# Two figures of an order model: the issue of wide transfers and matmuls of small tiles, in a two-branch decoder layer

## The chip, the cores and the metric

The kernel runs on one core of a Trainium2 chip. The metric is device time of one execution in microseconds. Three runs of the kernel before gave 1865.16, 1866.49 and 1883.88 us; the median is 1866.49 us.

## The reference

One hybrid decoder layer on 2048 positions of width 1024, batch 1, all in float32. The heart of it, cut:

```python
h = x_ln * (1 + scale(c)) + shift(c)          # layer norm, then modulation by c @ w_ada
proj = h @ w_in                               # 1024 -> 4232 columns
rw = proj[:, :1664]; rw = rw + (shifted(rw) - rw) * mix
# group A, RWKV-7, 8 heads x 64: per position
#   S = S * w_t - (S kk_t)(kk_t * a_t)^T + v_t k_t^T ;  y_t = S r_t
# then a group norm and a bonus term
# group B, forgetting attention, 8 heads x 64, causal, blocks of 128 queries:
#   softmax(q k^T / 8 + cum_t - cum_s) v
y = concat(y_a, y_b) * silu(proj[:, 3208:])
out = layer_norm(2 ** 0.25 * x_ln + (1 + gate(c)) * (y @ w_out)) * ln_g + ln_b
```

## The kernel before, in words

**Tiles.** The positions go in two halves of 1024, each half in two blocks of 512. The projection of a half is 33 weight tiles of 128 columns; each tile and block takes 8 steps over the inner dimension, and each step is three float32r matmuls of 128x128 by 512 columns (high times high, high times low, low times high; `proj_tile`). That makes 3,072 matmuls that read `ht` and `wsp`, besides 96 early ones that read `wx`. The output projection (`final_tile`) is 16 tiles of 128 positions with 48 such matmuls each, 768 in all; they read the same two names. These 3,840 matmuls depend on little: where one of them stands in TensorE's queue, it fills time that a chain would leave.

**Chains.** For each half there is a RWKV stage (`rwkv_stream`: 8 units, each with elementwise work, a triangular solve of small 32x32 matmuls, state steps of 128x64 matmuls, and a post step) and then an attention stage (`fox_stream`). In an attention stage `fox_ops` loads the operands of the heads (`fx_s`) from scratch in DRAM, `fox_guard` computes scores for the row maxima (a matmul into a bank of PSUM, then a reduction on VectorE that frees the bank; at most GI = 3 are in flight), `fox_s` computes the scores again for the exponentials (into `fx_p`), and `fox_pv` multiplies by the values (`fx_v`), two key tiles side by side on the halves of the array. `fox_values` transposes the values out of `arena` tiles that come from `vscr`. The stages are called attention 0 and attention 1 here.

**Ends.** `final_prep` loads `w_ada` and `w_out`, and VectorE and GpSimd scale `w_out` and split it into two parts (it starts when all projections of half 1 have been planned, and the parts take the place of half 1's activations, so when these have been used). Each output tile has an epilogue on VectorE: `final_evac` adds the residual, takes statistics and writes four passes over 128x512 (`SCALAR_TENSOR_TENSOR`), two of which can be read at the end of the program as `end_s<-end_s,small,arena`.

**What sets the order.** All instructions are recorded by generators that a small scheduler, `Driver`, runs in the order of a model's time. Each call of an engine asks `Driver.time`, which takes the cost from `cost` (or, for TensorE, `on_pe`, which keeps a time for each of the 4x4 cells of the array and adds 100 ns where the tile's shape changes) and notes when the result is ready. A generator that yields goes on when the model says that its work is done; free slots and banks are given out by the same clock. So a figure in the model changes no instruction but, by shifting the model's time, which generator goes next, and with it the place of every later instruction in the five in-order queues. The model's figure is never a time on the chip.

Names: `NB` is 512 columns, `pe.free` is when the model's TensorE is free, `LATENCY` is what the model adds behind each engine's end. All recorded instructions carry the line of the recording call (L134), so the profile is read by tile names.

Of the kernel before, what the change touches and what calls it, by code (L numbers as in the profile page):

```python
# [137 lines left out]
class Driver:  # L138
# [31 lines left out]
    def cost(self, e, op, ops, kw):  # L170
        out, ins = ops[0], ops[1:]
        n = max(a.free_size() for a in ops)
        sb = all(a.space != "PSUM" for a in ops)
        if "dma_start" in op:
            return 450.0 if e.name == "sp" else 1000.0
        if e.name == "act":
            return (94 if sb else 51) + 0.834 * n + 93 * sum(isinstance(kw.get(k), bass.AP) for k in ("scale", "bias"))
        if e.name == "dve":
            if op == "reciprocal":
                return 65 + 6.25 * n  # L180
            if op == "tensor_tensor_scan":
                return 69 + 2.15 * n
            if op == "tensor_tensor_reduce":
                return 180 + 1.04 * n
            ptr = 61 * sum(a.free_size() == 1 for a in ins[1:]) if "scalar" in op else 0
            if op in ("tensor_copy", "tensor_scalar", "memset") and sb:
                return 69 + 0.52 * n + ptr
            return 69 + 1.04 * n + ptr
        if op == "affine_select":
            return 137 + 0.834 * n  # L190
        if kw.get("op") == OP.pow:
            return 300 + 165 * n
        return 147 + 2.17 * n if op == "tensor_tensor" else 161 + 0.834 * n if op == "tensor_scalar" else 34 + 0.834 * n
# [17 lines left out]
    def on_pe(self, t, op, ops):  # L211

        m, n, k = ops[1].free_size(), ops[2].free_size(), list(ops[1].ap)[0][1]
        r0, c0 = ops[1].start_partition() // 32, ops[0].start_partition() // 32
        nr, nc = (1 if x <= 32 else 2 if x <= 64 else 4 for x in (k, m))
        one = ops[1].dtype == F32R or op == "transpose"
        stream, load = n * (1 if one else 2) / 2.4, m * 2 / 2.4
        if nr == nc == 4:
            d = max(stream + (14 if n >= 256 else 3), load + 2)
        else:  # L220
            d = max(stream + (load if nc < 4 else 6), 25.0)
        d *= 1 if one else 2
        t = max(t, self.pe.began + 7)
        if (nr, nc) != self.mode:
            t = max(t, max(max(x) for x in self.cells) + (100 if self.mode else 0))
            self.mode = (nr, nc)
        cells = [(i, j) for i in range(r0, min(4, r0 + nr)) for j in range(c0, min(4, c0 + nc))]
        t = max(t, max(self.cells[i][j] for i, j in cells))
        for i, j in cells:
            self.cells[i][j] = t + d  # L230
        self.pe.began = t + (0 if one else 7)
        self.pe.free = max(self.pe.free, t + d)
        return t + d
# [1871 lines left out]
```

## Time and profile before

| What | Value |
|---|---|
| Median of three runs | 1866.49 us |
| The profiled execution's own time | 1866.47 us |
| Its span | 1864.7 us |
| TensorE busy | 1784.5 us, 96% |
| VectorE busy | 1287.4 us, 69% |
| ScalarE busy | 804.4 us, 43% |
| GpSimd busy | 779.3 us, 42% |
| DMA, mean share of 16 engines | 30.6% |
| Granted TensorE clock, mean | 0.98 of 2.4 GHz |

The profiled execution is 0.02 us from the median, and 1.8 us of its time lie outside the span. A busy TensorE is not one at its peak: a matmul counts as busy from its start to its modelled end, and at a granted clock of 0.5 (1.2 GHz) it counts twice as long. A stretch's idle time is its length less TensorE's busy time.

### The profile page before, as it was taken

The numbers are of one execution on the slowest core, as the hardware profiler recorded it, in microseconds if no ns is written. First come the engines' busy times: TensorE is split into PE (matmuls) and PEld (weight loads), VectorE is DVE, ScalarE is ACT, GpSimd is POOL, SyncE is SP. The second block draws the span as 40 slices with busy tenths as digits, with TensorE's granted clock in tenths as the row PEclk, the third lists the DMA queues.
The fourth block names the chain that finished last, engine by engine and source line by source line (L and its number), as shares of the span: only waits on it lengthen the run. The fifth ranks groups of instructions, "written<-read, shape, count | busy, mean of one in ns | idle before, by whom it ended". The sixth has DMA issues, their size and how long they took to land.

```text
span 1864.7 us, 35565 instructions
## 1 busy us (share of the span) xinstructions
PE 1784.5 (96%) x13609; PEld 1288.3 (69%) x13609; DVE 1287.4 (69%) x3049; ACT 804.4 (43%) x1571; POOL 779.3 (42%) x773
## 2 busy tenths in 40 slices
PE   8999999999999899999999999989899899999995
PEld 6777777767777656677777777767555356666884
DVE  4987685665773768667657675762677584876998
ACT  2454555354444245554554554443244344432000
POOL 1333242422423357743143442424256364566652
PEclk8999999998999999999999999999899899999998
DMA  8252020210122755132021120213422732512433
GB/s 263 72 163 81 30 69 23 80 51 26 53 87 86 226 172 178 58 115 84 19 78 36 41 79 30 75 39 114 131 92 84 244 111 77 191 57 90 153 115 122
DMA packets 172129, 181.60 MB, mean 97 GB/s; under 512 B 12180, under 2 KB 116197, under 8 KB 171960
## 3 DMA queue, kind: packets, MB, share of 16 engines
q1 hardware_dynamic: 171960, 179.33, 30.6%
q8 instruction: 108, 1.77, 0.4%
q14 instruction: 61, 0.50, 0.1%
HBM read 132.10 MB, written 47.13 MB: 96 GB/s over the span
## 4 chain that ended last, share of the span: by engine, by line
PE 55%; DVE 5%; ACT 3%; SPq 3%; DMA 2%; issue 2%; POOL 1%; DVEq 0%; ACTq 0%; POOLq 0%
PE ps L134 55%; SPq L134 3%; ACT rw_s L134 2%; DVE rw_s L134 2%; DMA arena<-vscr 1%; DVE end_s L134 1%; DVE small L134 1%; DVE arena L134 1%; POOL rw_s L134 0%; POOL wsp L134 0%; DMA arena<-in_b_ada_dram 0%; ACT arena L134 0%; DMA yscr<-rw_s 0%; DVE fx_p L134 0%; DMA fx_s<-qscr 0%
## 5 line engine op out<-in xcount | busy, mean ns | idle before, releaser
L134 PE MATMUL ps<-ht,wsp 128*128 128x512 f32 x3840 | 976.4, 400 | 3.4 <-POOL wsp L134 1.3
L134 PEld LDWEIGHTS ps<-ht,wsp 128*128 128x128 f32 x3840 | 701.1, 189 | 163.3 <-issue 15.0
L134 POOL TENSOR_TENSOR wsp<-wst,wsp 128x1024 fp32r<-128x1024 f32 x79 | 192.8, 2440 | 320.2 <-ACT wsp L134 256.2
L134 ACT ACTIVATE rw_s<-ps 64x256 f32<-64x256 f32 (+3 forms) x544 | 215.9, 409 | 200.7 <-PE ps L134 101.0
L134 PE MATMUL ps<-fx_s 67*128 67x512 f32 (+6 forms) x960 | 261.1, 390 | 12.3 <-DMA fx_s<-kscr 4.0
L134 ACT ACTIVATE fx_p<-ps 128x512 f32<-128x512 f32 (+3 forms) x336 | 162.8, 521 | 196.2 <-PE ps L134 175.6
L134 PEld LDWEIGHTS ps<-fx_s 67*128 67x128 f32 (+1 forms) x960 | 165.4, 193 | 118.3 <-issue 47.7
L134 POOL TENSOR_TENSOR fx_p<-fx_p 128x512 f32<-128x512 f32 (+2 forms) x160 | 185.7, 1167 | 140.7 <-PE ps L134 138.3
L134 PE MATMUL ps<-rw_s 32*32 32x32 f32 (+4 forms) x5376 | 227.7, 217 | 17.0 <-DVE rw_s L134 8.0
L134 PEld LDWEIGHTS ps<-rw_s 32*32 32x32 f32 (+3 forms) x5376 | 195.7, 130 | 66.1 <-issue 26.6
L134 DVE TENSOR_TENSOR rw_s<-rw_s 128x24 f32<-128x24 f32 (+11 forms) x544 | 179.8, 336 | 26.0 <-ACT rw_s L134 12.6
L134 DVE TENSOR_REDUCE small<-ps 128x1 f32<-128x512 f32 (+1 forms) x208 | 134.5, 683 | 44.4 <-PE ps L134 43.6
L134 ACT ACTIVATE arena<-ps 128x512 f32<-128x512 f32 (+3 forms) x128 | 74.1, 581 | 191.6 <-PE ps L134 161.7
L134 POOL TENSOR_TENSOR small<-small,nhalf 128x8 f32<-128x8 f32 (+1 forms) x48 | 68.3, 1425 | 211.6 <-DVE small L134 211.5
L134 PE MATMUL ps<-fx_p,fx_v 128*64 128x512 f32 (+3 forms) x640 | 155.9, 556 | 0.0
L134 DVE TENSOR_TENSOR fx_p<-fx_p 128x512 f32<-128x512 f32 (+1 forms) x128 | 111.9, 874 | 51.6 <-POOL fx_p L134 48.9
L134 ACT ACTIVATE wsp<-wst 128x1024 fp32r<-128x1024 f32 x80 | 84.3, 1054 | 134.2 <-PE ps L134 110.1
L134 DVE TENSOR_SCALAR state<-ps,dl 64x64 f32<-64x64 f32 x256 | 72.4, 283 | 64.2 <-PE ps L134 57.2
L134 POOL TENSOR_TENSOR rw_s<-rw_s,arena 128x512 f32<-128x512 f32 x64 | 84.9, 1328 | 69.4 <-ACT arena L134 39.2
L134 DVE TENSOR_TENSOR arena<-ps,arena 128x512 fp32r<-128x512 f32 (+4 forms) x108 | 72.5, 677 | 54.0 <-ACT arena L134 50.3
L134 POOL TENSOR_SCALAR rw_s<-rw_s 64x128 f32<-64x128 f32 x128 | 38.0, 297 | 120.0 <-PE ps L134 109.4
L134 ACT ACTIVATE rw_s<-rw_s 32x256 f32<-32x256 f32 (+2 forms) x112 | 70.0, 653 | 39.4 <-DVE rw_s L134 38.7
(152 smaller groups left out, 1864.9 us busy)
## 6 DMA issues: line engine op xcount, KB each, us to landing
wst<-in_w_in_dram SPq DMA_DIRECT2D x66, 512.0 KB
fx_s<-kscr SPq DMA_DIRECT2D x144, 128.0 KB
fx_s<-qscr SPq DMA_DIRECT2D x96, 128.0 KB
ada_t<-in_w_ada_dram SPq DMA_DIRECT2D x16, 512.0 KB
rw_l<-lowscr SPq DMA_DIRECT2D x32, 256.0 KB
kscr<-arena SPq DMA_DIRECT2D x32, 256.0 KB
qscr<-arena SPq DMA_DIRECT2D x32, 256.0 KB
arena<-in_x_dram SPq DMA_DIRECT2D x16, 512.0 KB
```

The lines of the kernel that those rows point to most:

```text
L134: return fn(*args, **kw)
```

## The change

Two figures in the model become others; no line that records an instruction is touched.

```diff
@@ cost
         if "dma_start" in op:
-            return 450.0 if e.name == "sp" else 1000.0
+            return (450.0 if list(out.ap)[0][1] <= 8 else 600.0) if e.name == "sp" else 1000.0
@@ on_pe
         if nr == nc == 4:
             d = max(stream + (14 if n >= 256 else 3), load + 2)
         else:
-            d = max(stream + (load if nc < 4 else 6), 25.0)
+            d = max(stream + 6, load + 5, 52.0)
         d *= 1 if one else 2
```

`list(out.ap)[0][1]` is the number of rows (partitions) that a transfer writes. `stream` is the columns and `load` the weight columns in the model's ns; `one` is true for float32r, and float32 is counted twice. With these lines a float32 matmul of 128x64 tiles by 64 columns goes from 213 to 119 ns in the model, one of 128x64 by 512 columns from 960 to 865 ns, one of 32x32 by 16 columns from 80 to 104 ns; the full-array matmuls stay.

Both programs have 9,663 matmuls and the same other work. The orders differ from an early point on. Counted over TensorE's queue, the shape of the tile changes 1,035 times before and 1,055 times now. When the last matmul of RWKV half 0 is issued, 1,293 matmuls on `ht,wsp` have gone ahead of it before, 1,335 now; at the last of RWKV half 1 it is 2,781 before and 3,000 now.

First place: TensorE's queue where attention 0 begins, from the last transposes of the RWKV stage (`ident,rw_s`) to the first scores (`fx_s`); `ident,arena` are the transposes of the values, `ident,small` turns the maxima of a query block into a row. Before, and then now:

```order
L134 MATMUL ps<-ident,rw_s 128x128 x4
L134 MATMUL ps<-ht,wsp 128x512 x57
L134 MATMUL ps<-ident,arena 128x128 x4
L134 MATMUL ps<-ht,wsp 128x512 x6
L134 MATMUL ps<-fx_s 128x128
L134 MATMUL ps<-fx_s 128x256
L134 MATMUL ps<-fx_s 128x384
```

```order
L134 MATMUL ps<-ident,rw_s 128x128 x4
L134 MATMUL ps<-ht,wsp 128x512 x108
L134 MATMUL ps<-ident,arena 128x128 x4
L134 MATMUL ps<-ht,wsp 128x512 x6
L134 MATMUL ps<-fx_s 128x128
L134 MATMUL ps<-fx_s 128x256
L134 MATMUL ps<-fx_s 128x384
```

51 more projection matmuls stand between the two stages.

Second place: TensorE's queue in the first scores of attention 1. Before, and then now:

```order
L134 MATMUL ps<-fx_s 128x512 x3
L134 MATMUL ps<-ht,wsp 128x512 x3
L134 MATMUL ps<-fx_s 128x512
L134 MATMUL ps<-ht,wsp 128x512 x3
L134 MATMUL ps<-fx_s 128x512
L134 MATMUL ps<-ht,wsp 128x512 x3
L134 MATMUL ps<-fx_s 128x512 x2
L134 MATMUL ps<-ht,wsp 128x512 x3
L134 MATMUL ps<-fx_s 128x512
L134 MATMUL ps<-ht,wsp 128x512 x6
L134 MATMUL ps<-fx_s 128x128
```

```order
L134 MATMUL ps<-fx_s 128x512 x3
L134 MATMUL ps<-ht,wsp 128x512 x3
L134 MATMUL ps<-fx_s 128x512
L134 MATMUL ps<-ht,wsp 128x512 x3
L134 MATMUL ps<-fx_s 128x512 x4
L134 MATMUL ps<-fx_s 128x128
L134 MATMUL ps<-fx_s 128x256
L134 MATMUL ps<-fx_s 128x384
L134 MATMUL ps<-fx_s 128x512 x6
L134 MATMUL ps<-ident,small 4x128
L134 MATMUL ps<-fx_s 128x512 x7
```

Three projection matmuls stood behind nearly every score matmul; now the scores stand next to each other, and the projections have gone ahead into the RWKV stage. VectorE's queue has in this stretch, behind some 40 reductions, the scaling and splitting of `w_out` that before stood in the second half of attention 1. In SP's queue the transfers of `final_prep` that begin it, the row of `b_ada` and six of the eight `w_ada` tiles, now stand ahead of attention 1's first operands; before, all of them stood among the operands of its fifth and sixth heads.

Third place: the end of VectorE's queue (`small` are columns of statistics). Before, and then now:

```order
L134 SCALAR_TENSOR_TENSOR end_s<-end_s,small,arena 128x512
L134 TENSOR_TENSOR small<-small 128x1
L134 SCALAR_TENSOR_TENSOR end_s<-end_s,small,arena 128x512 x2
L134 TENSOR_SCALAR small<-small 128x1
L134 TENSOR_TENSOR small<-small 128x1
L134 SCALAR_TENSOR_TENSOR end_s<-end_s,small,arena 128x512 x2
L134 TENSOR_TENSOR small<-small 128x1 x2
L134 SCALAR_TENSOR_TENSOR end_s<-end_s,small,arena 128x512 x3
L134 TENSOR_SCALAR small<-small 128x1
L134 SCALAR_TENSOR_TENSOR end_s<-end_s,small,arena 128x512
L134 TENSOR_TENSOR small<-small 128x1
L134 SCALAR_TENSOR_TENSOR end_s<-end_s,small,arena 128x512 x7
```

```order
L134 TENSOR_TENSOR end_s<-ps,end_s 128x512
L134 TENSOR_TENSOR small<-small 128x1
L134 BN_STATS small<-end_s 128x6
L134 SCALAR_TENSOR_TENSOR end_s<-end_s,small,arena 128x512
L134 BN_AGGR small<-small 128x2
L134 SCALAR_TENSOR_TENSOR end_s<-end_s,small,arena 128x512
L134 TENSOR_SCALAR small<-small 128x1
L134 SCALAR_TENSOR_TENSOR end_s<-end_s,small,arena 128x512 x2
L134 TENSOR_TENSOR small<-small 128x1 x2
L134 TENSOR_SCALAR small<-small 128x1
L134 TENSOR_TENSOR small<-small 128x1
L134 SCALAR_TENSOR_TENSOR end_s<-end_s,small,arena 128x512 x5
```

Behind the last instruction that takes a result out of PSUM (`end_s<-ps,end_s`) stood 22 wide passes and 2 statistics (the rows shown are the last of them); now 9 wide passes and 1 statistic stand there. 546 matmuls on `ht,wsp` came behind attention 1 before, 384 do now: four output tiles or so have moved ahead.

## Rows read from the trace of the kernel before

**Rows 1.** The page: the span, busy time by engine, the chain by engine.
```profile
span 1864.7 us, 35565 instructions
PE 1784.5 (96%) x13609; PEld 1288.3 (69%) x13609; DVE 1287.4 (69%) x3049; ACT 804.4 (43%) x1571; POOL 779.3 (42%) x773
PE 55%; DVE 5%; ACT 3%; SPq 3%; DMA 2%; issue 2%; POOL 1%; DVEq 0%; ACTq 0%; POOLq 0%
```

**Rows 2.** Windows: start:end, length, busy PE, PEld, DVE, ACT, POOL, clock, DMA, GB/s.
```profile
400.00:450.00 50.00, 46.76 (x590) 35.76 (x589) 27.02 (x95) 26.59 (x60) 10.14 (x16) 0.86 0.04 12
...
600.00:650.00 50.00, 45.16 (x204) 32.95 (x202) 30.95 (x90) 13.92 (x32) 13.56 (x17) 0.97 0.71 224
...
1300.00:1350.00 50.00, 42.40 (x171) 29.75 (x170) 29.66 (x65) 11.64 (x23) 10.88 (x7) 0.90 0.49 149
...
1450.00:1500.00 50.00, 44.84 (x200) 21.54 (x199) 31.27 (x56) 17.39 (x36) 19.53 (x20) 0.86 0.72 244
...
1750.00:1800.00 50.00, 50.00 (x222) 41.42 (x221) 47.20 (x66) 4.25 (x4) 35.72 (x17) 1.00 0.36 121
1800.00:1850.00 50.00, 43.95 (x194) 36.05 (x193) 47.10 (x86) 3.18 (x3) 19.46 (x12) 0.99 0.31 107
```

**Rows 3.** SP's queue in order of time, start of attention 0: start, length, instruction.
```profile
605.94 1.24 SPq L134 DMA_DIRECT2D fx_s<-qscr  x2
607.22 2.51 SPq L134 DMA_DIRECT2D fx_s<-kscr  x4
...
613.16 0.45 SPq L134 DMA_DIRECT2D fx_s<-cscr  x1
```

**Rows 4.** The chain that ended last: start, length, what; three transfers in it.
```profile
628.91 9.10 DMA arena<-vscr
...
1325.26 6.29 DMA arena<-vscr
...
1451.92 6.85 DMA arena<-in_b_ada_dram
```

**Rows 5.** TensorE in order of time, start of attention 1 ([idle before it <-releaser]).
```profile
1307.72 0.40 PE L134 MATMUL ps<-fx_s 67*128 67x512 f32 x1
1307.96 0.86 PE L134 MATMUL ps<-ht,wsp 128*128 128x512 f32 x3
1308.66 0.40 PE L134 MATMUL ps<-fx_s 67*128 67x512 f32 x1
...
1331.68 0.66 PE L134 MATMUL ps<-ident,arena 128*128 128x128 f32 x2 [6.06 <-DMA arena<-vscr]
```

**Rows 6.** VectorE in order of time: start of attention 1, and the end.
```profile
1306.77 3.08 DVE L134 TENSOR_REDUCE small<-ps 128x1 f32<-128x512 f32 x5 [16.35 <-PE ps L134]
...
1843.99 0.69 DVE L134 TENSOR_TENSOR end_s<-ps,end_s 128x512 f32<-128x512 f32 x1 [2.51 <-PE ps L134]
...
1845.52 1.27 DVE L134 BATCH_NORM_STATS2 small<-end_s 128x6 f32<-128x512 f32 x2
...
1856.98 4.72 DVE L134 SCALAR_TENSOR_TENSOR end_s<-end_s,small,arena 128x512 f32<-128x512 f32 x7
```

**Rows 7.** Groups by shape: busy us, mean ns of one, idle before.
```profile
L134 PE MATMUL ps<-fx_p,fx_v 128*64 128x512 f32 x448 | 139.2, 623 | 0.0
...
L134 DVE TENSOR_TENSOR fx_p<-fx_p 128x512 f32<-128x512 f32 x96 | 89.7, 935 | 48.3 <-POOL fx_p L134 46.3 <-ACT fx_p L134 0.9
...
L134 DVE TENSOR_TENSOR ht<-arena,ht 128x512 fp32r<-128x512 f32 x24 | 24.7, 1031 | 11.4 <-ACT ht L134 11.3
...
L134 DVE TENSOR_TENSOR arena<-arena 128x512 f32<-128x512 f32 x16 | 15.4, 975 | 0.2 <-DMA arena<-in_w_out_dram 0.2
```

**Rows 8.** TensorE in order of time, a state step between projections.
```profile
1280.38 0.34 PE L134 MATMUL ps<-state,rw_s 128*64 128x64 f32 x4
1280.55 0.29 PE L134 MATMUL ps<-rw_s,state 128*64 128x64 f32 x4
1280.77 1.66 PE L134 MATMUL ps<-ht,wsp 128*128 128x512 f32 x6
```

## The prediction

> **What bounds the kernel now.** The page comes first: TensorE is busy for 1784.5 of 1864.7 us, and 55% of the chain that ended last is TensorE's own work, while no other engine holds more than 5% of it [rows 1]. So the time is TensorE's work, which the change leaves as it is, plus the time in which it stands still or runs at its lower clock. The windows say where that is [rows 2]. From 600 to 650 us (the start of attention 0) it is busy for 45.16 us, so 4.8 us are idle, and the granted clock is 0.97. From 1300 to 1350 (the start of attention 1) 7.6 us are idle at a clock of 0.90; from 1450 to 1500 it is 5.2 us at 0.86; from 400 to 450 (RWKV) 3.2 us at 0.86; and from 1800 the work runs out before the span does. The clock has two levels, 2.4 and 1.2 GHz, so 0.86 over 50 us means 14 us at the lower one, which costs 7 us where TensorE had work; 0.90 costs 5 us and 0.97 costs 1.5 us in the same way.
>
> What the stalls wait for is in the chain of waits. At both starts of an attention stage it holds a transfer of values, 9.10 and 6.29 us long; the one that begins at 1451.92 is a row of `b_ada` [rows 4]. SP's queue shows why the values are late: operands of the heads are issued one behind another, two in 1.24 us, four in 2.51 us, and a row of three partitions in 0.45 us [rows 3]. That is about 0.62 us for a wide transfer, so the new 600 is the better figure than 450, and 450 stays right for 3 rows.
>
> **The change, part by part.** Nothing is added or removed. What moves is the order, and I read the price of it at four places.
>
> *Start of attention 0.* 51 more projection matmuls stand between the last RWKV transposes and the first transposes of values. Three of them took 0.70 us between two scores (1307.96 to 1308.66) [rows 5], so 51 are 11.9 us of work in front of the stage. They lie exactly where SP is issuing and the values are on their way. The 4.8 us of idle time and the 1.5 us of clock from 600 to 650 [rows 2] are less than this cover, so nearly all goes: I take -5 us, between 0 (the second transfer of values still stands behind 42 operand transfers, and a wait for it would only come later) and -6.3.
>
> *Start of attention 1.* Here the cover is taken away. Before, a score (0.24 us) and three projections (0.70 us) stood together, 0.94 us for each bank (1307.72 to 1308.66) [rows 5], and VectorE reduced a bank in 3.08 / 5 = 0.62 us [rows 6]; TensorE was the slower one and did not wait. Now the scores stand bare, and with three banks in flight TensorE must go at VectorE's pace. Counted in the two queues from the first score to the point at which VectorE is furthest behind: VectorE has 40 reductions at 0.62 us, 24.6 us; 16 masked ones, on average of 320 columns, 0.3 to 0.6 us each, say 7.5; 15 scalings of `w_out` at 0.975 and 8 splits at 1.031 [rows 7], 22.9; 9 sums of `fx_p` at 0.935 [rows 7], 8.4; 7 others of 512 columns, at 0.65 some 4.5. That makes 67.9 us. TensorE has 88 scores at 0.24 us, 21.1 us; 22 narrower ones, say 3; 32 projections, 7.5; 24 products with the values, for which the group's busy time is 139.2 us over 448 instructions, two to a matmul, 0.62 us [rows 7], and no less than 0.4 if two run side by side, so 10 to 15; some 2 of small ones. That makes 43 to 49 us. VectorE is over by 19 to 25 us, and by 12 if its `w_out` passes took 0.67 us, as the last seven wide passes do [rows 6]. I take 20 us, since the means are of passes that ran in the same company as now.
>
> Against this stands what goes. The wait of 6.06 us for values [rows 5] may stay: the second transfer of values again stands behind more than 40 operand transfers. But TensorE is now late by itself and meets it late; I leave 3 us of it. The stall at 1450 goes: the row of `b_ada` and six of the eight `w_ada` tiles are now asked for before attention 1, under projections. Together the two windows hold 7.6 + 5.0 + 5.2 + 7.0 = 24.8 us of idle time and clock [rows 2], some of it counted twice where TensorE was idle at the lower clock; I take 20. So this place gives 20 + 3 - 20 = +3 us, between 12 - 24.8 = -13 and 25 + 6 - 12.8 = +18.
>
> *End.* TensorE's last result leaves PSUM at 1843.99, and VectorE's last seven passes end near 1861.7 after 4.72 us, 0.67 us a pass [rows 6]. Behind that last result stood 22 passes and 2 statistics, now 9 and 1. That is 13 x 0.67 + 0.6 (half of 1.27 us [rows 6]) = 9.3 us less. It holds if VectorE is not further behind by then: it has 47 of 50 us from 1750 on [rows 2] with four more output tiles to finish than now. I take -9 us, between -4 and -9.3.
>
> *Small tiles.* The tile's shape changes 20 times more. A visit to the 128x64 shape lasts 0.39 us from its first matmul to the next projection (1280.38 to 1280.77), its own work included [rows 8], so a change costs at most half of it: 0 to 4 us for 20, and I take +2.
>
> In the RWKV stages I count nothing: the chains there have the same steps, and the fillers between two state steps are as many or more.
>
> **The sum.** -5 + 3 - 9 + 2 = -9 us. The profiled execution took 1866.5 us (span 1864.7 and 1.8 outside), the median to 0.02 us, so I predict 1857 us.
>
> **The rivals.** (a) *Attention 1 becomes VectorE's* (slower). With 219 more projections spent before the end of RWKV half 1, nothing fills the first scores. For it: VectorE's queue is over by 19 to 25 us, and behind it come stretches with no filler at all. Against it: in attention 1 TensorE was busy without idle time at few projections once products stood in its queue. It decides as soon as VectorE's excess is more than the 20 us that go. With +25, the whole wait of 6 and only the 12.8 us of idle time gone it is +18; and while TensorE is fed by a third of its time its clock may fall, as it did in the windows with idle time from 1300 and 1450 [rows 2], for 14 us at the lower level, 7 us. Then 1866.5 + 18 + 7 - 5 + 2 = 1888. The Trainium skill, page "TensorE: Matmul & The Clock Gate", Part 1, says that the array is throttled by default and that activity releases it. By that rule the fall comes; the windows agree as far as they go, since each clock below 1.00 listed stands with idle time of 1 us or more. Chance 0.17.
>
> (b) *The better figures repay in RWKV too.* If the waits go that the model did not see there, the window from 400 gives back up to 3.2 + 7.0 us [rows 2], and attention 1 comes out near the middle of its lower half, -5 instead of +3: 1857 - 10 - 8 = 1839. For it: the new figure for issues is near the rows. Against it: the RWKV stages issue few transfers, and stalls of a few us arise anew in any order. Chance 0.22.
>
> (c) *Nothing to measure.* The stalls move and add up to the same; TensorE's work decides: 1866, within 7. For it: 1784.5 us of busy time cannot change [rows 1]; against it: the end, which is plain in the queue. Chance 0.21. That the change does nothing at all is excluded by the orders.
>
> **Chances and range.** The forecast, 1849 to 1866, has 0.40, (a) 0.17, (b) 0.22, (c) 0.21. About 1%, 18.7 us, can be told from no change here. Faster by more than that (under 1848): (b) and a little of the forecast, 0.24. Slower (over 1885): most of (a), 0.15. Within: 0.61. The range that leaves out 2 in 10 goes from 1838, near the middle of (b), to 1882, where half of the upper bounds of attention 1 are taken in.
>
> **What would show it.** Right: the stretch before attention 0 without idle TensorE; the second scores of attention 1 with TensorE waiting on VectorE, VectorE over 90% busy for some 60 us there, and no stall on `b_ada`; less than 12 us from the last PSUM result to the end. Wrong: a clock below 0.9 over attention 1's start and idle time of over 35 us there (a); RWKV windows with under 1 us of idle time each (b); a last result from PSUM with VectorE still two tiles behind. What would make it wrong most easily is a wait that no row shows: a transfer or bank late in the new order in a place where the old one had it in time.

## The result and the profile after

The changed kernel takes 1882.39 us (median of 20 runs), the kernel before 1865.18 us on the same chip: a ratio of 1.0079, interval 1.0057 to 1.0101. (Ratios are of means, here without one execution of 1901.06 us that fell into a slower state; the medians differ by 17.2 us.) It is some 15 us slower, just above the range's upper end and on the other side of the forecast. The profiled execution of the changed kernel spans 1880.2 us, 15.5 more than before.

The page of the changed kernel, the lines that answer to [rows 1] (span; TensorE's line; the chain by engine):

```profile
span 1880.2 us, 35546 instructions
PE 1803.7 (96%) x13609; PEld 1289.5 (69%) x13609; DVE 1277.2 (68%) x3049; ACT 803.8 (43%) x1571; POOL 773.9 (41%) x773
PE 23%; DVE 3%; DMA 2%; SPq 1%; issue 0%; POOL 0%; ACT 0%; ACTq 0%; POOLq 0%; DVEq 0%
```

TensorE is busy 19 us longer with the same matmuls. It stood at the lower clock for 96 us, before for 74, which makes up to 11 us of it; for the rest, a busy TensorE is not one at its peak. Windows of the changed kernel (columns as in [rows 2]); first the places that [rows 2] has, then four short ones at the start of attention 1:

```profile
400.00:450.00 50.00, 48.91 (x686) 38.98 (x685) 35.56 (x107) 22.93 (x48) 11.20 (x14) 1.00 0.11 31
600.00:650.00 50.00, 47.56 (x240) 35.96 (x238) 36.54 (x95) 17.71 (x31) 15.50 (x11) 1.00 0.81 258
1350.00:1400.00 50.00, 42.93 (x151) 21.42 (x151) 40.50 (x75) 18.79 (x38) 22.74 (x17) 0.82 0.58 192
1450.00:1500.00 50.00, 49.79 (x242) 30.13 (x241) 39.05 (x79) 17.61 (x33) 29.28 (x29) 1.00 0.34 104
1750.00:1800.00 50.00, 39.98 (x177) 30.28 (x177) 27.42 (x46) 4.39 (x7) 23.96 (x17) 0.86 0.34 111
...
1340.00:1350.00 10.00, 7.97 (x25) 4.67 (x24) 10.00 (x23) 0.86 (x2) 0.00 (x0) 0.87 0.60 194
1350.00:1355.00 5.00, 4.95 (x11) 2.76 (x11) 5.00 (x14) 0.00 (x0) 0.00 (x0) 0.50 0.47 147
1355.00:1360.00 5.00, 2.13 (x6) 0.78 (x4) 4.79 (x10) 0.00 (x0) 0.00 (x0) 0.50 0.74 218
1360.00:1365.00 5.00, 1.42 (x5) 0.60 (x9) 0.58 (x1) 1.21 (x2) 1.55 (x1) 0.50 0.93 337
```

RWKV and attention 0 are better than before (48.91 against 46.76 at 400, 47.56 against 45.16 at 600) and the stall at 1450 is gone; attention 1 begins worse, and from 1750 there is a hole of 10 us that was not there.

To add such places up, I use one measure throughout: a stretch's **loss** is its length less what its matmuls take at the pitch of their kind, from start to start, where TensorE neither waits nor runs at the lower clock in the trace of before (for the 128x128x512 ones on `ht,wsp`, called tile matmuls below, 0.227 us; at the lower clock they keep 0.427). The work comes to some 1745 us in every kernel, since the matmuls are the same. Another mean of the pitch moves a column by up to 13 us for all kernels alike, and the differences between kernels by 1 us or so: read the differences. Losses in us, in brackets the tile matmuls in the stretch; "start" is from attention 1's first own matmul to its first product with values, "heads" are cut at the products of each head, "seam" is from attention 1's last own matmul to the last matmul of all, "drain" is what comes behind that.

| Profiled execution | Ahead of attention 1 | Start | Heads 0-3 | Heads 4-5 | Heads 6-7 | Seam | Drain |
|---|---|---|---|---|---|---|---|
| before | 82.5 | 7.4 (57) | 6.3 (39) | -3.2 (141) | 3.5 (207) | -0.1 (545) | 20.8 |
| changed | 62.7 | 16.2 (6) | 6.7 (276) | 16.4 (12) | 6.0 (96) | 13.1 (383) | 11.5 |
| difference | -19.8 | +8.8 | +0.4 | +19.6 | +2.5 | +13.2 | -9.3 |

The sum is +15.4. So three places in and behind attention 1 cost 42 us, and two gains of 29 us stand against them. Each row is one execution, timed executions of one kernel lie up to 26 us apart, and a profiled one up to 11 us from its kernel's median; a few us in one cell say nothing.

**The start.** The chain that ended last, changed kernel, around 1350 (start, length, what):

```profile
1331.16 5.30 DMA fx_s<-qscr
...
1351.57 0.45 SPq L134
1352.07 0.45 SPq L134
1352.56 0.59 SPq L134
...
1356.45 5.85 DMA wst<-yscr
1362.32 1.06 ACT wsp L134
1363.38 0.17 ACT mrow L134
1363.58 4.49 PE ps L134 x14
```

From 1336.48 to 1355.72 the chain is SP alone: 34 operand transfers of the heads, issued one behind another in 19.2 us. Then comes the transfer for the first output tile's weights, and in order of time one sees whom it holds:

```profile
1347.71 6.06 DVE L134 TENSOR_REDUCE small<-ps 128x1 f32<-128x512 f32 x10
...
1362.32 1.06 ACT L134 ACTIVATE wsp<-wst 128x1024 fp32r<-128x1024 f32 x1 [13.79 <-DMA wst<-yscr]
1363.28 0.25 ACT L134 ACTIVATE mrow<-ps 4x128 fp32r<-4x128 f32 x1
...
1363.58 0.29 PEld L134 LDWEIGHTS ps<-fx_s 67*128 67x128 f32 x1 [6.22 <-ACT mrow L134]
1363.58 0.79 PE L134 MATMUL ps<-fx_s 67*128 67x512 f32 x1 [5.50 <-ACT mrow L134]
```

ScalarE sits 13.79 us in front of the weights' cast, and the row of maxima, for which the scores wait, stands behind it in its queue. TensorE has nothing else.

**Heads 4 and 5.** What TensorE waited for there (1582 to 1675):

```profile
PE ps L134 <- DMA arena<-vscr: 1.8, 1, 1.8
PE ps L134 <- ACT fx_p L134: 1.4, 2, 0.7
PE ps L134 <- DMA fx_s<-mrow: 1.3, 1, 1.3
PE ps L134 <- DVE small L134: 0.4, 1, 0.4
```

4.9 us of waits; and in three falls from 1593 on the clock was at its lower level for 20.5 us, which costs 10.2. That is 15.1 of the 16.4. Not all of it is the order's: e3, e13 and e14 below have the same order here and wait in the same places, for 4.8 to 5.1 us, but their clock was at the lower level for 3.4 to 6.8 us alone, and they lose 10.2 to 12.0. So these heads cost 13 to 20 us, and the row has the worst of four executions. The longest wait is one for values again: their transfer goes out at 1632.95, behind operands of the heads that SP has been issuing since 1623.15.

**The seam.** Changed kernel, in order of time:

```profile
1765.66 2.33 PE L134 MATMUL ps<-ht,wsp 128*128 128x512 f32 x9
1767.83 0.60 PE L134 MATMUL ps<-ident,fx_p 128*128 128x128 f32 x4
...
1770.69 0.32 SPq L134 DMA_DIRECT2D yscr<-arena  x1
1771.66 0.41 SPq L134 DMA_DIRECT2D wst<-yscr  x1
1776.14 1.06 ACT L134 ACTIVATE wsp<-wst 128x1024 fp32r<-128x1024 f32 x1 [10.90 <-DMA wst<-yscr]
...
1777.25 1.22 PE L134 MATMUL ps<-ht,wsp 128*128 128x512 f32 x2 [8.82 <-ACT wsp L134]
```

Attention's last result is stored at 1770.69, the first output tile of half 1 reads it back as weights, and TensorE waits 8.82 us for them. The clock is at its lower level for 13.65 us behind it. Before, 3.4 output tiles of half 0 (545 - 383 = 162 tile matmuls, 37 us) still stood here.

**The end.** VectorE's last sum from PSUM and its last passes, where [rows 6] had 1843.99 and 1856.98:

```profile
1868.79 0.68 DVE L134 TENSOR_TENSOR end_s<-ps,end_s 128x512 f32<-128x512 f32 x1
...
1873.58 3.64 DVE L134 SCALAR_TENSOR_TENSOR end_s<-end_s,small,arena 128x512 f32<-128x512 f32 x5
```

### The profile page after: what moved, and what is told of

Read it like the earlier page. It is cut to its first block, busy times and chain, and to the rows that moved or that the text cites. A ratio compares the mean times of both kernels' runs of the same rounds, so it can differ in the third digit from the quotient of the medians.

```text
span 1880.2 us, 35546 instructions
## 1 busy us (share of the span) xinstructions
PE 1803.7 (96%) x13609; PEld 1289.5 (69%) x13609; DVE 1277.2 (68%) x3049; ACT 803.8 (43%) x1571; POOL 773.9 (41%) x773
## 5 line engine op out<-in xcount | busy, mean ns | idle before, releaser
L134 PE MATMUL ps<-fx_s 67*128 67x512 f32 (+5 forms) x960 | 266.5, 397 | 16.0 <-ACT mrow L134 5.5
L134 DVE TENSOR_TENSOR rw_s<-rw_s 128x24 f32<-128x24 f32 (+11 forms) x544 | 174.1, 326 | 21.9 <-ACT rw_s L134 9.3
L134 PE MATMUL ps<-fx_p,fx_v 128*64 128x512 f32 (+3 forms) x640 | 167.6, 569 | 1.2 <-ACT fx_p L134 0.9
L134 DVE TENSOR_TENSOR arena<-ps,arena 128x512 f32<-128x512 f32 (+4 forms) x108 | 72.8, 678 | 100.8 <-ACT arena L134 84.5
L134 DVE TENSOR_TENSOR fx_p<-fx_p 128x512 f32<-128x512 f32 (+1 forms) x128 | 108.0, 844 | 21.7 <-POOL fx_p L134 19.4
L134 PEld LDWEIGHTS ps<-fx_p,fx_v 128*64 128x64 f32 x640 | 41.7, 139 | 59.2 <-issue 38.3
```

What stands on the lines that cost most here:

```text
L134: return fn(*args, **kw)
```

## The experiments

Three theories. *Cover*: the time is lost where chains stand without tile matmuls, because the new order spends them earlier. *Scatter*: every new order draws new stalls, whatever cover it keeps. *Small tiles*: the small tiles themselves cost more in the new order. Ratios are to the kernel before on the same chip.

**e1 and e2: each figure alone.** One changed line taken back in each.

> Only the figure for transfers is changed (600 for more than 8 rows); the figure for small tiles is the old one. By its order the last RWKV stage spends 1,062 matmuls of projection or output tiles, as before the change (changed kernel: 1,233); attention 1 holds 486 (before 444, changed 390), the stretch behind it 504 (546, 384). Cover theory (the 15 us are lost where attention 1 and its end have no such matmuls left): attention 1 starts covered and output tiles are left for its end, so 1862 to 1870, no stall of over 3 us at the seam behind attention 1. Scatter theory (each new order draws new stalls, whatever cover it keeps): anything from 1850 to 1890. Small-tile theory (denser or more numerous small tiles cost the time): as before, 1865, since that figure is the old one.

> Only the figure for small tiles is changed; transfers have the old one. By its order the last RWKV stage spends 1,161 projection and output matmuls (before 1,062, changed 1,233), attention 1 holds 510, of which 126 are projections at its start, and all eight output tiles of half 0 are gone at its end, as in the changed kernel. Cover theory: the seam behind attention 1 stalls as in the changed kernel (8 to 9 us idle and some 14 us at the lower clock, +13), the drain is short (-9), attention 1's start is half covered (+5 to +10), and the gains ahead of attention 1 stay (-10 to -15): 1868 to 1880. Scatter theory: anything from 1850 to 1890. Small-tile theory: all of the loss, 1880 to 1884.

Measured: e1 1868.51 us, ratio 1.0007 (0.9989 to 1.0026): nothing. e2 1857.53 us, 0.9956 (0.9939 to 0.9973): faster, so the small-tile theory falls, and the cover theory's range was too high as well, by 10. Neither figure alone makes the loss; e2's losses are 60.7 ahead, 14.0 (42) at the start, -0.1 (135) in heads 4 and 5, 16.5 (383) at the seam. Most of what sets e2 apart from the changed kernel lies in heads 4 and 5: 123 more tile matmuls, and 16.5 us less lost.

**e3: cover for the seam.**

```diff
                 it, w = wready.popleft()
+                while it[2] in (6, 7) and "pvdone" not in flag:   # set behind fox_pv's last matmul
+                    yield 0
```

> The changed kernel, with the last two output tiles of half 0 (96 matmuls, 21.8 us of work) held until attention 1 has issued its last product with values; all ahead of that stays in the same order. Cover theory: the 8.8 us without work at the seam and most of the 13.7 us at the lower clock behind it go, -10 to -14, and up to +4 comes back where the two tiles ran before: 1868 to 1876, with less than 2 us idle at the seam. Scatter theory: a stall of the same size turns up elsewhere, 1878 to 1888. If the seam waits for something that its cover does not reach (the weights' chain starts later by as much), no change: 1880 to 1884.

Measured: 1873.89 us, 1.0045 (1.0025 to 1.0065), as the cover theory had it. The seam's loss is -0.1 (443) instead of 13.1. The total shows 6 us of that by the ratios and 8.5 by the medians: heads 6 and 7, from which the tiles were taken, lose some 3 us more, and the drain 2.

**e4: tiles withheld from the last RWKV stage.**

```diff
+            while 66 - 6 <= n < 66 and "att1" not in flag:        # set behind rwkv_stream(1)
+                yield 0
```

> The changed kernel, with the last 6 projection tiles (288 matmuls) held back until the last RWKV stage has issued everything; the RWKV stage then spends 1,017 such matmuls (before 1,062, changed 1,233), attention 1 holds 444 (444, 390), the stretch behind it 558 (546, 384). Cover theory: the stretch from attention 1's first operand to its first product with values loses 7 us of excess instead of 16, heads 4 and 5 lose nothing instead of 16, the seam nothing instead of 13, the drain is 20 us again instead of 11.5; the last RWKV stage loses its gain of 5 us: 1850 to 1866 in all. Scatter theory: no place of attention 1 is better on the whole, 1870 to 1890. Small-tile theory: the figures are the changed ones, so 1880 to 1884.

Measured: 1891.82 us, 1.0143 (1.0118 to 1.0167): the total is far off. At the places that it names the theory held: start -0.2 (69), heads 4 and 5 0.5 (138), seam 1.2 (557); heads 0 to 3 lost some 5 more than in the changed kernel. But the loss ahead went from 62.7 to 107.2. The RWKV stage had no tile matmul in its last 60 us (the changed kernel 168), and it had its own chains to cover. Windows of e4 there:

```profile
1260.00:1280.00 20.00, 7.08 (x179) 4.99 (x180) 12.68 (x49) 4.32 (x9) 6.18 (x8) 0.58 0.04 14
1280.00:1300.00 20.00, 15.68 (x174) 13.40 (x165) 5.21 (x20) 7.85 (x21) 1.18 (x4) 0.59 0.01 2
```

TensorE is busy for 7.08 of 20 us. A tile matmul kept for later is taken from somewhere; here the place that it was taken from lost more.

**e5 to e8: other places for the same tiles.** e5 is e2 with e3's hold. e6 hands out one half-0 tile for each head whose scores are issued. e7 and e8 change one number, which shifts the order by itself:

```diff
-            return (450.0 if list(out.ap)[0][1] <= 8 else 600.0) if e.name == "sp" else 1000.0
+            return (450.0 if list(out.ap)[0][1] <= 8 else 650.0) if e.name == "sp" else 1000.0   # e8: 700.0
```

> Only the figure for small tiles is changed, and the last two output tiles of half 0 are held until attention 1 has issued its last product with values. Candidate for a version that beats both. Seam part of the cover theory: in the kernel with that figure alone the seam cost 10.6 us without work and 17 us at the lower clock; the 33 matmuls that now stand behind (7.5 us) leave some 3 us of it, and the clock holds: 1843 to 1850. If the seam is not what these tiles cover: 1855 to 1860. Scatter theory: a stall of the same size elsewhere, 1852 to 1865.

> The changed kernel, with the output tiles of half 0 handed out one for each head whose scores are issued (six of them), the last two behind the last product with values; all up to attention 1 stays in the same order. Matmuls of output tiles by head are 39, 42, 54, 39, 45, 60, 9, 0 (changed kernel: 33, 87, 93, 63, 12, 0, 0, 51), 18 and 462 behind (45, 384). Cover theory: heads 4 and 5 lose 0 to 4 us instead of 16, the seam 0 instead of 13, heads 6 and 7 up to 10 more, the drain 4 more; at attention 1's start the weights of the first output tile are no longer ahead of the row of maxima on ScalarE, so that its 5.5 us without work go unless another transfer takes that place: 1852 to 1868. Scatter theory: 1874 to 1890.

> The changed kernel with 650 in place of 600 for transfers of more than 8 rows. Its order spends 1,110 projection and output matmuls in the last RWKV stage (changed kernel 1,233) and has 102 at attention 1's start (6), by head 0, 15, 27, 54, 93, 51, 75, 57 (33, 87, 93, 63, 12, 0, 0, 51); all half-0 output tiles are gone at the seam, as in the changed kernel. Cover theory: start and heads 4 and 5 lose 0 to 5 us instead of 32, the seam 13 to 17 as before: 1848 to 1862. Theory that a dearer figure for transfers is itself what costs: 1882 or more. Scatter theory: no tie to these counts, 1850 to 1890.

> The changed kernel with 700 in place of 600 for transfers of more than 8 rows. Its order spends 1,269 matmuls of projection and output tiles in the last RWKV stage (changed kernel 1,233) and leaves 9 for attention 1's start (6); by head 21, 72, 42, 60, 51, 42, 0, 51 (33, 87, 93, 63, 12, 0, 0, 51), 39 and 390 behind. Cover theory: the start costs what it costs in the changed kernel (16 to 21), the seam too (13 to 16), but heads 4 and 5, now with 51 and 42, lose 0 to 4 instead of 16: 1862 to 1874. Theory that the dearer figure costs by itself: above 1882. Scatter theory: 1850 to 1890.

Measured: e5 1850.01 us, 0.9907 (0.9887 to 0.9928); e6 1858.74, 0.9951 (0.9927 to 0.9974); e7 1855.89, 0.9933 (0.9910 to 0.9957); e8 1858.51, 0.9960 (0.9942 to 0.9978). e6 and e7 fell where cover put them, e5 at the very end of it, e8 3.5 us below. By place: e7's start lost 2.1 (102), e8's 14.9 (9), e6's 12.4 (12); heads 4 and 5 lost -2.4 (105) in e6, 3.9 (144) in e7, -1.3 (93) in e8. So it is not the size of the figure (650 and 700 are faster than 450 and 600) but which tiles its order leaves where. TensorE at e7's start, in order of time, where the changed kernel had scores alone:

```profile
1312.77 0.62 PE L134 MATMUL ps<-fx_s 67*128 67x512 f32 x2
1313.23 1.55 PE L134 MATMUL ps<-ht,wsp 128*128 128x512 f32 x6
1314.62 0.40 PE L134 MATMUL ps<-fx_s 67*128 67x512 f32 x1
1314.85 0.86 PE L134 MATMUL ps<-ht,wsp 128*128 128x512 f32 x3
```

**e9: no output tile before the last head.**

```diff
-    HB = 6
+    HB = 0
```

> The changed kernel with no output tile of half 0 let out before the scores of the last head: heads 0 to 6 of attention 1 stand without any projection or output matmul (changed kernel: 33, 87, 93, 63, 12, 0, 0), head 7 has 54, and 60 and 654 stand behind. All up to attention 1 keeps its order. Bare-head theory (a head without such matmuls loses some 8 us, as heads 4 and 5 of the changed kernel did): seven bare heads lose 45 to 60, the seam nothing, the drain is 20 to 22: 1895 to 1915. Trail theory (heads 4 and 5 lost time because VectorE was still working off the six output tiles, whose matmuls were already spent; a bare head with nothing of that beside it loses nothing, as heads 0 to 2 before): the heads lose -5 to +6 in all, the start 16, the seam 0, the drain 20 to 22: 1841 to 1856.

Measured: 1862.40 us, 0.9959 (0.9937 to 0.9981). The bare-head theory falls: heads 0 to 6 have no tile matmul at all, and heads 4 and 5 lose -2.7, with no wait of TensorE listed there (1512 to 1583). The median lies 6 us above the trail theory's range, the profiled execution (span 1849.5) within it. A bare head is cheap if its own order has no wait in it; e9's head 0, bare too, waits 4.2 us for an operand, and heads 0 to 3 lost some 10 us.

**e10 and e11: the figure for small tiles, halved.** New for at most 128 columns in e10, for more in e11; the rest old.

> Of the change, only the figure for tiles below 128x128 with at most 128 columns (the small tiles of the RWKV stages, and the sums); products with values and transfers keep the old ones. Its order spends 1,275 projection and output matmuls in the last RWKV stage (changed kernel 1,233, before 1,062) and leaves 6 at attention 1's start, by head 36, 96, 90, 48, 18, 0, 0, 57, then 39 and 384: nearly what the changed kernel has. Cover theory: gains of 20 to 24 ahead of attention 1, and the same losses as in the changed kernel behind: 1870 to 1884. Theory that the two figures must come together for the loss: 1855 to 1868, as with the figure for small tiles alone.

> Of the change, only the figure for tiles below 128x128 with more than 128 columns (the products with values of attention); the small tiles of the RWKV stages and transfers keep the old ones. Its order spends 1,062 projection and output matmuls in the last RWKV stage, as before, with 57 at attention 1's start, by head 9, 9, 12, 18, 9, 141, 54, 72, then 72 and 537, as before too. Cover theory: no gain ahead of attention 1 and no loss in it: 1860 to 1870. Theory that attention's own figure brings the gains: 1840 to 1855.

Measured: e10 1886.77 us, 1.0107 (1.0076 to 1.0138), 3 us above the range; e11 1870.83, 1.0013 (0.9991 to 1.0035), 1 above. The loss is there without the figure for transfers, once the small tiles' figure alone leaves the same places bare: start 18.9 (6), seam 16.5 (383). e10's heads 4 and 5 lost only 2.5 (18), its heads 0 to 3 14.3 (270). The gain ahead of attention 1 goes with the small tiles' figure as well: 70.8 in e10, 80.3 in e11. Over all kernels, those with it lost 54 to 74 there (e4 apart), those without it 80 to 93.

**e12, e15, e17: versions that could beat both.** e12: 650 and a hold for tiles 5 to 7; e15: 700 and e6's pacing; e17: e2 and a hold for tiles 5 to 7.

> The kernel with 650 for transfers of more than 8 rows, and the last three output tiles of half 0 (144 matmuls, 32.7 us of work) held until attention 1 has issued its last product with values. Candidate for a version that beats both. Seam part of the cover theory: its seam cost 15.3 us (11.8 without work), all of which goes; head 7, now bare, loses up to 5; the drain stays at 12 to 14: 1841 to 1850. If the weights of the first tile of half 1 come later by as much as the cover is longer: 1853 to 1860.

> The kernel with 700 for transfers of more than 8 rows, with output tiles of half 0 handed out one for each head whose scores are issued, the last two behind the last product with values. Matmuls by head: 30, 54, 36, 57, 39, 30, 39, 3, then 42 and 438. Candidate for a version that beats both. Cover theory: ahead of attention 1 as in the kernel with 700 (54 of excess), start 15, heads 0 to 5 5 to 8, heads 6 and 7 8 to 12, seam 0, drain 12: 1840 to 1850. Scatter theory: 1850 to 1870.

> Only the figure for small tiles is changed, and the last three output tiles of half 0 (144 matmuls, 32.7 us) are held until attention 1 has issued its last product with values; 54 and 474 matmuls then stand behind (kernel with two held: 63 and 417, 9.2 us lost at the seam). Candidate for a version that beats both. Cover theory: the seam loses nothing, head 7, now bare, 2 to 5 more, the drain is 12 to 15: 1842 to 1849. If the weights of the first tile of half 1 come later by as much: 1850 to 1855.

Measured: e12 1851.13 us, 0.9893 (0.9867 to 0.9919); e15 1856.19, 0.9926 (0.9900 to 0.9952); e17 1848.76, 0.9907 (0.9886 to 0.9929). All beat both kernels; e12, e17 and e5 cannot be told apart, although e5 still lost 9.2 (416) at its seam: heads 6 and 7 and the drain give back some 4 us in e17, the rest is not accounted for. e17 is in its range, e12 1 above. e15 missed by 6 and lies in the scatter theory's range: its seam closed, but heads 0 to 5 lost 16.8 where 5 to 8 were expected. All three lose -0.1 at the seam. e12's seam, in order of time:

```profile
1730.75 14.58 PE L134 MATMUL ps<-ht,wsp 128*128 128x512 f32 x63
...
1735.62 0.38 SPq L134 DMA_DIRECT2D wst<-yscr  x1
...
1741.38 1.06 ACT L134 ACTIVATE wsp<-wst 128x1024 fp32r<-128x1024 f32 x1 [14.87 <-DMA wst<-yscr]
```

The way of the weights is as long as before; 63 tile matmuls now lie over it.

**e13, e14, e16: VectorE's work made narrow, every instruction in its place.** The model still charges the full width, so that the orders stay.

```diff
+            if self.drv.cut and self.name == "dve":      # set around the ops named
+                args = [narrow(a) for a in args]         # a[:, 0:64]
             return fn(*args, **kw)
```

> The changed kernel with every instruction on every engine in its place; VectorE's instructions on the output tiles 0 to 5 of half 0 (sums with the residual, statistics, scaling) work on 64 columns instead of 512 or 1,024, so that these tiles' results are left incomplete. Trail theory (heads 0 to 5 lose 23 us in the changed kernel, 3 before, because VectorE works on the output tiles beside its reductions): the heads lose 3 to 10, 1864 to 1873. Bare-head or clock theory (they lose it whatever VectorE does): 1878 to 1884.

> The changed kernel with every instruction on every engine in its place; the maxima of the off-diagonal score tiles of heads 0 and 1 in attention 1 are taken over 64 columns instead of 512, so that the shift of these heads' exponents is of a part of the scores only. VectorE-pace theory (the prediction's): the stretch from the first operand to the first product with values loses 3 to 8 us instead of 16, and the clock falls for less than 10 us there instead of 20: 1868 to 1876. Transfer theory (the start waits for one transfer that ScalarE's queue has ahead of the row of maxima): the same 5 to 6 us without work at the end of the reductions, the row only waits longer; 12 us or more lost: 1877 to 1884.

> The kernel of e9 (no output tile of half 0 before the last head) with every instruction in its place; the maxima of the off-diagonal score tiles of heads 0 and 1 in attention 1 are taken over 64 columns instead of 512, so that the shift of these heads' exponents is of a part of the scores only. In e9 ScalarE writes the first rows of maxima at once and VectorE is busy without a break up to there. VectorE-pace theory, now that no weights stand ahead: the stretch from the first operand to the first product with values loses 2 to 7 us instead of 12.4, 1852 to 1858. Transfer theory (SP issues some 26 operand transfers one after the other and the row of maxima stands behind them): the stretch loses 10 to 15, 1859 to 1866.

Measured: e13 1879.65 us, 1.0046 (1.0026 to 1.0066); e14 1879.67, 1.0057 (1.0039 to 1.0076); e16 1860.67, 0.9964 (0.9944 to 0.9984), the same as e9. VectorE's pace is out as the bound of the start: with reductions of 0.22 us each instead of 0.68 it loses 22.4 in e14 and 17.5 in e16, more than with wide ones. e14, in order of time:

```profile
1351.93 0.39 SPq L140 DMA_DIRECT2D wst<-yscr  x1
...
1358.36 1.06 ACT L140 ACTIVATE wsp<-wst 128x1024 fp32r<-128x1024 f32 x1 [18.25 <-DMA wst<-yscr]
1359.33 0.25 ACT L140 ACTIVATE mrow<-ps 4x128 fp32r<-4x128 f32 x1
...
1359.63 0.79 PE L140 MATMUL ps<-fx_s 67*128 67x512 f32 x1 [9.65 <-ACT mrow L140]
```

(L140 is this file's line for every recorded instruction.) The faster VectorE only waited longer for the same transfer, which went out 18.6 us after the first score, in the changed kernel 17.6. In e16, without output weights there, TensorE's own queue stops instead, at the matmuls of the gate (`final_prep`):

```profile
1357.27 1.92 PE L140 MATMUL ps<-arena,ct 128*32 128x512 f32 x4 [5.93 <-DMA arena<-in_w_ada_dram]
```

e13 leaves heads 4 and 5 at 11.3 us; e3 and e14, which have the same order there and full-width epilogues, lost 10.2 and 12.0. Of TensorE's waits the one on VectorE is gone, the others stand (1580 to 1667):

```profile
PE ps L140 <- DMA arena<-vscr: 2.2, 1, 2.2
PE ps L140 <- ACT fx_p L140: 1.4, 2, 0.7
PE ps L140 <- DMA fx_s<-mrow: 1.3, 1, 1.3
```

So VectorE's epilogues are not shown to be the cause either. By the ratios e13 lies 6 us under the changed kernel, but the intervals overlap.

## Why the prediction was wrong, point by point

The step that failed is the price of the tile matmuls that the new order spends early. The prediction priced their absence in one place, attention 1's start, and there by VectorE's pace. It put heads 4 to 7 and the way from attention 1 to the output tiles of half 1 at nothing, and booked the shorter tail as a gain alone. The start cost 8.8 us more, by another path; heads 4 and 5 cost 13 to 20 us and the seam 13.2. Rival (a) had the direction and a fall of the clock, but through VectorE's excess, which e14 does not bear out.

**Attention 0, -5.** Right in kind: the loss of that stage goes from 9.8 to 6.6 us, -3.2, and the other kernels with this order lost 6 to 8. Between the two stages TensorE was idle for nothing, but before too (0.1 us); what went lies behind, 2.4 instead of 4.8 us idle in the 60 us from the last RWKV matmul. The cover between the stages is not enough for it: e2, e7 and e10 have 19 to 27 us there (before 15) and lost 3 to 7 us more than before in the stage.

**RWKV, nothing.** Wrong. The losses of the two RWKV stages go from 33.4 to 24.3 and from 28.6 to 22.8 us, -15 together. That was the mechanism of rival (b), which I had at 10. That it comes with the figure for small tiles is shown (e2, e10 against e1, e11); how it acts inside these stages I did not try.

**Start of attention 1, +3: the path that I had wrong.** I wrote that TensorE must go at VectorE's pace. VectorE looks like it, 10.00 of 10 and 5.00 of 5 us busy up to 1355, though not for 60 us; but a busy engine is the bound only if what follows it could go earlier, and e14 shows that it couldn't. By the chain the pace was SP's: 34 issues in 19.2 us, then one transfer that ScalarE's queue stood behind, and TensorE behind that. I had those rows [rows 3] and used them for the figure, not for the path. The stretch lost 8.8 us more than before because 6 tile matmuls instead of 57 lay over it (with 69 in e4 it lost nothing): over all kernels here, a start with 57 to 102 of them lost -0.3 to 7.8 us, one with 6 to 42 lost 12.4 to 22.4. The Trainium skill, page "Trainium Kernel Development and Optimization", Key Constraints, says that issuing transfers from several engines saves only the sequencer's issue time; here that time, 19.2 us, is the chain. No run issued them from a second queue, so what that would gain is not shown.

The clock fell with it: 0.50 from 1347.5 on for 20.5 us, after the first waits, where the forecast had no fall and rival (a) had 14 us of it. The Trainium skill, page "TensorE: Matmul & The Clock Gate", Part 1, has the array throttled unless activity releases it; the windows agree (from 1355 to 1360, at 0.50, TensorE is busy for 2.13 of 5 us).

**The stalls that go, -20.** The one on `b_ada` at 1450 went, as said (busy 49.79 of 50). But heads 0 to 3 lose 6.7 against 6.3: other small waits took its place.

**What no term had: heads 4 and 5, +19.6.** Rival (a) names "stretches with no filler at all" and gives them no price of their own. Against them it set that TensorE was busy without idle time in attention 1 at few projections. The waits and the clock are shown above; the kernels with 93 tile matmuls or more in these heads lost -3.2 to 3.9 us (e2, e6, e7 and e8 among them). That bareness alone is not the cause is shown by e9. What makes this one order wait where e9's does not stays open, and so does why its clock fell for 20.5 us in one execution and 3.4 in another; VectorE's epilogues are at most a few us of it (e13). Here the scatter theory keeps a part: with 18 tile matmuls or fewer these two heads lost anything from -2.9 to 16.4 us (e16, e9, e10, e3, e13, e14, the changed kernel), while the start and the seam follow their counts.

**The end, -9.** Right to 0.3 us: the drain went from 20.8 to 11.5. But the four output tiles that left the tail had another use, which I did not price: they covered the way from attention's last store to the next weights. That cost 13.2 us at the seam, shown by e3, e12 and e17, and it is the wait "in a place where the old one had it in time" of my last sentence. In all kernels, a tail of 437 tile matmuls or more lost -0.2 to 1.2 us there, one of 383 to 416 lost 9.2 to 16.5.

**Small tiles, +2.** Not seen. e4 has 1,017 changes of shape and is the slowest, e9 has 1,063 and beats the kernel before.

**The sum.** Ahead of attention 1 I was 15 us too high, at its start and in heads 0 to 3 6 too low (+9.2 against +3), in heads 4 to 7 and at the seam 35 too low, and 2 too high for the small tiles: 24 in all.

## What to carry to other kernels

Work that depends on little is a store: when a better cost figure spends it earlier, list the places that lived on it, and price each of them bare, the far ones (the end of a stage, the way through DRAM into the next) above all. When an engine looks full, ask what else the work behind it waits for; a chain of issues on one queue does not show in any engine's busy time. Two figures of which neither costs time alone (e1, e2) can together give a worse order, so time them one by one.

## What the runs showed of the hardware

How long SP takes to issue a transfer depended on the one ahead of it as well as on its own rows. In the changed kernel's start, transfers of 64 rows and 128 KB took 0.45 us each where they alternated with transfers of 3 rows, which took 0.45 us too, and 0.59 us each behind one of their own kind; the first of a row of four took 0.45 (the chain above, at 1352.07 and 1352.56):

```profile
1351.08 0.44 SPq L134 DMA_DIRECT2D fx_s<-kscr  x1
1351.57 0.45 SPq L134 DMA_DIRECT2D fx_s<-cscr  x1
1352.07 2.36 SPq L134 DMA_DIRECT2D fx_s<-qscr  x4
```

So 450 or 600 by the transfer's own rows alone is not what the queue does, though the prediction took the new figure for the better one: a wide transfer behind a narrow one took no longer than the narrow one.
